# 1/rms by one power instruction and one Newton step, in a two-layer encoder kernel

## The chip, the cores and the metric

The kernel runs on one core of a Trainium2 chip. The metric is device time in microseconds (us) of one execution; the kernel before has a median of 1916.23 us over 3 runs (1915.28 to 1917.49). Engines are named as in the profile: PE (TensorE matmul; PEld is its weight load), DVE (VectorE), ACT (ScalarE), POOL (GpSimd), SP (SyncE, which here issues the DMAs).

## The reference

A trunk of two layers is applied to a prompt of 512 rows and a sample of 1024 rows, each row 1024 wide, with shared weights. Layer 0 has two attentions side by side (A: grouped queries with axial rotary; B: a difference of two softmaxes, with an RMS norm on its output). Layer 1 has one, C, with three dilated windows. Each layer:

```python
def rms_norm(x, g):
    x32 = x.astype(jnp.float32)
    y = x32 * lax.rsqrt(jnp.mean(x32 * x32, axis=-1, keepdims=True) + EPS)
    return (y * g.astype(jnp.float32)).astype(x.dtype)
...
    h = rms_norm(x, norm_g)
    z = h @ w_in                                   # q, k, v and a gate, split by columns
    q = partial_rope(rms_norm(q.reshape(B, S, C_HEADS, HEAD_DIM), c_q_norm))
    k = partial_rope(rms_norm(k.reshape(B, S, C_HEADS, HEAD_DIM), c_k_norm))
...
    return x + (o * jax.nn.silu(gate)) @ w_out
```

So 1/sqrt(mean + eps) is wanted in three places: once per row for h; once per row and head for q and k; and once per row and head for the output of B. All of it is float32 to the outside. EPS is 1e-6.

## The kernel before

**Tiles.** Rows are taken 128 at a time (12 tiles), and grouped in three granules of 4 tiles (`GRAN`: the prompt, and two halves of the sample). Activations and weights are split into a high and a low fp16 half, so that a product takes three fp16 passes (`PASSES`). h is written as such a pair, transposed by a DMA into `hT`, and kept for the whole layer. The layer is worked off in 8 units of two heads. For each unit and granule `kv_piece` and `qg_piece` project k, v and q, gate (48 matmuls per pair of tiles, PSUM tiles `pj`), and `att_A`, `att_B` or `att_C` do the attention: scores `S` on PE, maximum on DVE, exponential on ACT, high and low half on ACT and DVE, a transposing DMA `t<-h`, and the product with V on PE. `out_tile` is the output projection.

**1/rms.** Each of the three places takes the sum of squares, scales it and adds eps, makes a first guess by integer arithmetic on the bits of the number (a multiplication by -0.5 and an addition of a magic constant), and improves it with three Newton steps of four instructions each (`newton`, L261 to L264):

- h, per tile or pair of tiles (`l0_h`, and `fin0` for layer 1; tile name `hs4`): `h_var` on DVE (L363 and the guess at L256), then 12 instructions on POOL. For the very first tile all 14 are on DVE. `h_split` then multiplies the tile by 1/rms (DVE, L374), and splits it (ACT L379, DVE L383).
- q and k (`qk_stages`; tile name `qs`, 128 rows by 8 values), 87 times: `f_red` sums on DVE (L527), `f_chain` puts 16 instructions on POOL: the square of the weight scale (L532, its tile is `wiz`), scale and eps (L533), guess (L534), Newton, and the weight scale again (L537). DVE then multiplies (`f_rope`, L568, or `f_r`, L560 for A), ACT and DVE split, and a transposing DMA puts K or q in place.
- the output of B (`att_B`, `fin`; tile name `bf`, 128 by 4), 12 times: scale and eps (L1046), guess (L1047), Newton, and two more instructions, all on POOL.

**Weight chunks.** `wprep` loads 256 columns of weights, sums their squares on ACT, adds them over partitions on PE (L436), makes a power of two of it on DVE (`f_pw`; the inverse scale goes to `wiz`, L447), and splits the weights (ACT L471, DVE L476). 29 chunks belong to w_in0 and w_in1, 8 to the output weights.

**Order.** A planner (`Plan`) sets the order of all instructions. Every stage is added with an engine and an estimated duration, e.g. `add("POOL", 6.9, f_chain, [s])`; `Plan.run` plays the stages through with these durations, and emits a stage when the modelled engine becomes free and its inputs are ready. Each engine then runs its instructions in the emitted order, SP its DMAs too. So a changed duration in an `add` changes the order on all engines. The list `START` orders the ramp, `END` the last two units.

Of the kernel before, what the change touches and what calls it, by code (L numbers as in the profile page):

```python
# [13 lines left out]
I32 = mybir.dt.int32  # L14
# [198 lines left out]
def trunk_kernel(ctx: ExitStack, tc: tile.TileContext, A: dict, outs: list):  # L213
# [186 lines left out]
    def wprep(w, cols, ih=None, iz=None, kinds=("whl",), deps=(), keep=2):  # L400
# [47 lines left out]
        pw = add("DVE", 0.75, f_pw, [mm] if ih is None else [mm, box["gst", 0 if w is w0 else 1]], (), [pt])  # L448
# [66 lines left out]
    def qk_stages(zb, ztok, evs, iz, tabs, tdep, ti, kind, isq, dst, dst_acq, dst_use, swap, dst_dep=()):  # L515
# [9 lines left out]
        def f_red():  # L525
            b["s"] = small(32, "qs", 6)
            V.tensor_reduce(out=b["s"][:, 0:8], in_=b["t1"].rearrange("p h t d -> p (h t) d"), op=AD, axis=AX.X)  # L527
        s = add("DVE", dve(512), f_red, [s], (), [t1t])

        def f_chain():  # L530
            x = b["s"]
            G.tensor_scalar(out=x[:, 24:25], in0=iz(), scalar1=iz(), scalar2=1.0 / 64, op0=M, op1=M)  # L532
            G.tensor_scalar(out=x[:, 8:16], in0=x[:, 0:8], scalar1=x[:, 24:25], scalar2=EPS, op0=M, op1=AD)  # L533
            G.tensor_scalar(out=x[:, 16:24].bitcast(I32), in0=x[:, 8:16].bitcast(I32), scalar1=-0.5, scalar2=MAGIC,  # L534
                            op0=M, op1=AD)
            newton(G, x[:, 16:24], x[:, 0:8], x[:, 8:16])
            G.tensor_scalar(out=x[:, 0:8], in0=x[:, 16:24], scalar1=iz(), scalar2=4096.0, op0=M, op1=M)  # L537
        sr = add("POOL", 6.9, f_chain, [s])
# [86 lines left out]
    def kv_piece(u, gi):  # L625
# [68 lines left out]
        u.k_ready[gi] = qk_stages(zb, ztok, evs, lambda: u.kvw.iz[:, 0:1], lambda: u.ktab, u.tdep, t0, u.kind, False,  # L694
# [1028 lines left out]
```

## Time and profile before

| | |
|---|---|
| median of 3 runs | 1916.23 us |
| the profiled execution, its own time | 1908.2 us |
| its span (first to last instruction) | 1906.3 us |
| mean granted clock of TensorE | 0.958 |
| PE busy | 1675.6 us (88%) |
| DVE, ACT, POOL busy | 1324.2 (69%), 1213.3 (64%), 862.0 us (45%) |
| PE at the start | first weight sum at 11.51 us, first projection at 21.41 us |

The span is the time from the first instruction to the last in one profiled execution; the execution's own time is 1.9 us longer, and the median of the timed runs 8.0 us above that. PE is the busiest engine; what it idles (1906.3 - 1675.6 = 230.7 us) is made of waits for other engines and for DMAs.

### The profile page before, as it was taken

What the parts mean: (1) busy time and instruction counts of PE and PEld (TensorE: products, weight loads), DVE (VectorE), ACT (ScalarE), POOL (GpSimd) and SP (SyncE); (2) the same over time, 40 slices, a digit from 0 to 9 for tenths busy, and PEclk for the clock granted to TensorE, in tenths of its full rate; (3) what the DMA queues carried; (4) which work ended last, traced back from release to release, by engine and by line L of the source; (5) the groups of instructions that cost most, each with busy time, mean ns of one, the idle gap of its engine ahead of it and who ended that gap; (6) DMA issues with size and microseconds to landing.
All of it is one profiled execution on the core that took longest, in us unless ns stands there. A gap on an engine that the chain in (4) does not pass through costs nothing.

```text
span 1906.3 us, 45950 instructions
## 1 busy us (share of the span) xinstructions
PE 1675.6 (88%) x17626; PEld 1400.0 (73%) x17626; DVE 1324.2 (69%) x2976; ACT 1213.3 (64%) x2593; POOL 862.0 (45%) x2272
## 2 busy tenths in 40 slices
PE   4588889999988999786899998999998889894898
PEld 3475667778877877465788887878887778783787
DVE  5768878877787778974555768676866767687432
ACT  4548878876676677753435668576767657786310
POOL 3743434444555575523124445554554564463100
PEclk9898999999999999897999999999999999997999
DMA  8678999995564554579787568484858666777983
GB/s 244 147 141 149 168 178 171 152 170 125 96 133 74 104 114 103 123 182 203 200 192 168 101 122 170 105 178 102 167 114 154 123 119 130 153 140 156 216 221 111
DMA packets 788734, 282.14 MB, mean 148 GB/s; under 512 B 647073, under 2 KB 772257, under 8 KB 788513
## 3 DMA queue, kind: packets, MB, share of 16 engines
q1 hardware_dynamic: 788512, 279.19, 71.2%
q8 instruction: 138, 2.26, 0.5%
q14 instruction: 84, 0.68, 0.1%
HBM read 73.92 MB, written 25.17 MB: 52 GB/s over the span
## 4 chain that ended last, share of the span: by engine, by line
PE 49%; DMA 10%; DVE 9%; ACT 5%; POOL 4%; issue 4%; SPq 2%; DVEq 0%; POOLq 0%; ACTq 0%
PE pj L490 36%; DMA t<-h 7%; PE pj L785 5%; PE S L773 3%; DVE f L1100 2%; PE S L1125 2%; DMA f<-in_w_in_dram 1%; PE pj L504 1%; DVE h L801 1%; ACT f L1110 1%; DVE whl L476 1%; PE S L1173 1%; DVE qs L527 1%; SPq L358 1%; ACT f L1025 1%
## 5 line engine op out<-in xcount | busy, mean ns | idle before, releaser
L490 PE MATMUL pj<-whl,hT 128*128 128x256 f16 x7680 | 882.5, 275 | 34.7 <-DMA hT<-h 31.9
L490 PEld LDWEIGHTS <-hT 128*128 128x128 f16 x7968 | 781.1, 99 | 152.8 <-DMA hT<-h 33.7
L785 PEld LDWEIGHTS <-t 128*128 128x128 f16 x4992 | 204.4, 101 | 105.0 <-DMA t<-h 91.8
L490 PEld LDWEIGHTS <-t 128*128 128x128 f16 x2304 | 229.0, 100 | 54.2 <-DMA t<-h 24.1
L1110 ACT ACTIVATE f<-f,cs,csc 128x256 f32<-128x256 f32 (+1 forms) x384 | 218.8, 574 | 60.5 <-DVE cs L779 60.2
L801 DVE TENSOR_TENSOR h<-f,h 128x1024 f16<-128x1024 f32 x148 | 186.4, 1262 | 78.7 <-ACT h L797 77.5
L773 PE MATMUL S<-K,q 128*128 128x512 f16 x640 | 173.1, 404 | 61.1 <-ACT f L1025 29.4
L490 PE MATMUL pj<-whl,t 128*128 128x256 f16 x1728 | 202.1, 279 | 23.2 <-DMA t<-h 23.2
L785 PE MATMUL pj<-V,t 128*128 128x64 f16 (+1 forms) x4032 | 181.3, 204 | 38.4 <-DMA t<-h 37.9
L797 ACT ACTIVATE h<-f 128x1024 f16<-128x1024 f32 x168 | 176.1, 1054 | 13.2 <-DMA t<-h 9.9
L773 PEld LDWEIGHTS <-q 128*128 128x128 f16 x640 | 62.5, 103 | 122.5 <-issue 63.6
L533 POOL TENSOR_SCALAR qs<-qs 128x8 f32<-128x8 f32 x87 | 41.1, 473 | 218.6 <-DVE qs L527 208.3
L1335 DVE SCALAR_TENSOR_TENSOR f<-pj,os,f 128x256 f32<-128x256 f32 x96 | 41.9, 479 | 114.4 <-PE pj L490 114.0
L855 DVE TENSOR_REDUCE as<-S 128x1 f32<-128x1024 f32 (+1 forms) x80 | 96.5, 1219 | 22.4 <-PE S L773 22.1
L424 ACT ACTIVATE t<-f 128x1024 bf16<-128x1024 f32 x74 | 77.9, 1053 | 49.3 <-DMA f<-in_w_in_dram 32.6
L865 ACT ACTIVATE f<-S,as,asc 128x1024 f32<-128x1024 f32 (+1 forms) x96 | 101.7, 1061 | 11.2 <-DVE h L801 6.1
L476 DVE SCALAR_TENSOR_TENSOR whl<-f,wsm,whl 128x1024 f16<-128x1024 f32 x68 | 89.0, 1325 | 11.4 <-ACT whl L471 11.1
L801 POOL TENSOR_TENSOR h<-f,h 128x1024 f16<-128x1024 f32 x20 | 45.3, 2264 | 96.8 <-ACT h L797 42.6
L471 ACT ACTIVATE whl<-f,wsm 128x1024 f16<-128x1024 f32 x68 | 76.2, 1144 | 19.2 <-PE pj L490 18.8
L1019 DVE TENSOR_REDUCE bs<-S 128x1 f32<-128x1024 f32 x64 | 77.3, 1217 | 15.4 <-PE S L773 15.2
L655 ACT ACTIVATE z<-pj 128x256 f32<-128x256 f32 x78 | 29.3, 376 | 92.0 <-PE pj L490 91.9
L262 POOL TENSOR_TENSOR qs<-qs 128x8 f32<-128x8 f32 x261 | 74.0, 284 | 20.4
(253 smaller groups left out, 2955.5 us busy)
## 6 DMA issues: line engine op xcount, KB each, us to landing
f<-in_w_in_dram SPq DMA_DIRECT2D x58, 512.0 KB, 5.1
mixbuf<-sg SPq DMA_DIRECT2D x48, 256.0 KB, 2.7
f<-mixbuf SPq DMA_DIRECT2D x24, 512.0 KB, 5.1
K<-K SPq DMA_DIRECT2D x78, 128.0 KB, 2.8
f<-in_w_out_dram SPq DMA_DIRECT2D x16, 512.0 KB, 5.3
pn<-pk SPq DMA_DIRECT2D x96, 66.0 KB, 2.5
x1buf<-f SPq DMA_DIRECT2D x12, 512.0 KB, 4.3
Vc<-V SPq DMA_DIRECT2D x96, 64.0 KB, 2.4
```

The costliest lines, as they stand in the source:

```text
L424: S_.activation(out=junk1(t1t), in_=b[i].rearrange("p k n -> p (k n)"), func=AF.Square, accum_out=b["s"][:, i:i + 1])
L471: S_.activation(out=part(k, 0, i), in_=b[i][:, nk * k:nk * k + nk, :], func=AF.Copy, scale=sc())
L476: stt(out=part(k, 1, i), in0=b[i][:, nk * k:nk * k + nk, :], scalar=sc(), in1=part(k, 0, i), op0=M, op1=SU)
L490: T.matmul(ps, lhs(k, a), wt(k, b), start=(k == 0 and i == 0), stop=(k == 7 and i == 2))
L773: T.matmul(out[:, 512 * i:512 * i + 512], q, u.K[:, st, gi, hk, :], start=(st == 0), stop=(st == 1))
L785: T.matmul(o, t4[:, 8 * a + base + k, :], v(k, b), start=(k == 0 and i == 0), stop=(k == nk - 1 and i == 2))
L797: S_.activation(out=b["hl"][:, 0, :], in_=b["e"], func=AF.Copy)
L801: (G if on_pool else V).tensor_tensor(b["hl"][:, 1, :], b["e"], b["hl"][:, 0, :], SU)
L855: V.tensor_reduce(out=b["s"][:, 0:nh], in_=b["S"].rearrange("p (h k) -> p h k", h=nh), op=ALU.max, axis=AX.X)
L865: S_.activation(out=b["e"][:, w * i:w * i + w], in_=b["S"][:, w * i:w * i + w], func=AF.Exp, bias=b["s"][:, 2 + i:3 + i], scale=u.sc, accu ...
L1019: V.tensor_reduce(out=b["s"][:, c:c + 1], in_=b["S", c], op=ALU.max, axis=AX.X)
L1110: S_.activation(out=b["e"][:, w * i:w * i + w], in_=b["e"][:, w * i:w * i + w], func=AF.Exp, bias=b["s"][:, i:i + 1], scale=u.sc, accum_ou ...
```

## The change

The guess and three Newton steps become one `pow` with exponent -0.5 on POOL (a constant tile `mhalf` holds the exponent) and one Newton step. In q and k the weight scale no longer enters per piece: `f_pw` works out eps divided by the square of the scale (`c.e2`, two DVE instructions per chunk of w_in), and the chain becomes six instructions. The two instructions of `h_var` go from DVE to POOL, and the first tile's whole chain too. The durations given to the planner follow.

```diff
-    def newton(eng, y, t, v):
-        for _ in range(3):
-            eng.tensor_tensor(t, y, y, M)
-            eng.tensor_tensor(t, t, v, M)
-            eng.tensor_scalar(out=t, in0=t, scalar1=-0.5, scalar2=1.5, op0=M, op1=AD)
-            eng.tensor_tensor(y, y, t, M)
+    def rsqrt(y, t, v, n):
+        G.tensor_tensor(y, v, mhalf[:, 0:n], ALU.pow)
+        G.tensor_tensor(t, y, y, M)
+        G.tensor_tensor(t, t, v, M)
+        G.tensor_scalar(out=t, in0=t, scalar1=-0.5, scalar2=1.5, op0=M, op1=AD)
+        G.tensor_tensor(y, y, t, M)
...
-    def h_var(s, n, eng):
-        ts(out=s[:, 0:n], in0=s[:, 0:n], scalar1=1.0 / D, scalar2=EPS, op0=M, op1=AD)
-        seed(s[:, n:2 * n], s[:, 0:n])
-        if eng is not None:
-            newton(eng, s[:, n:2 * n], s[:, 2 * n:3 * n], s[:, 0:n])
+    def h_rms(s, n):
+        G.tensor_scalar(out=s[:, 0:n], in0=s[:, 0:n], scalar1=1.0 / D, scalar2=EPS, op0=M, op1=AD)
+        rsqrt(s[:, n:2 * n], s[:, 2 * n:3 * n], s[:, 0:n], n)
...
                 ts(out=c.iz, in0=s[:, 4:4 + n], scalar1=ih(), scalar2=1.0 / P14, op0=M, op1=M)
-        pw = add("DVE", 0.75, f_pw, [mm] if ih is None else [mm, box["gst", 0 if w is w0 else 1]], (), [pt])
+                c.e2 = small(1, "we2", 12)
+                V.reciprocal(out=s[:, 4:5], in_=c.iz[:, 0:1])
+                ts(out=c.e2, in0=s[:, 4:5], scalar1=s[:, 4:5], scalar2=EPS / 4096.0 ** 2, op0=M, op1=M)
+        pw = add("DVE", 1.1, f_pw, [mm] if ih is None else [mm, box["gst", 0 if w is w0 else 1]], (), [pt])
...
         def f_chain():
             x = b["s"]
-            G.tensor_scalar(out=x[:, 24:25], in0=iz(), scalar1=iz(), scalar2=1.0 / 64, op0=M, op1=M)
-            G.tensor_scalar(out=x[:, 8:16], in0=x[:, 0:8], scalar1=x[:, 24:25], scalar2=EPS, op0=M, op1=AD)
-            G.tensor_scalar(out=x[:, 16:24].bitcast(I32), in0=x[:, 8:16].bitcast(I32), scalar1=-0.5, scalar2=MAGIC,
-                            op0=M, op1=AD)
-            newton(G, x[:, 16:24], x[:, 0:8], x[:, 8:16])
-            G.tensor_scalar(out=x[:, 0:8], in0=x[:, 16:24], scalar1=iz(), scalar2=4096.0, op0=M, op1=M)
-        sr = add("POOL", 6.9, f_chain, [s])
+            G.tensor_scalar(out=x[:, 8:16], in0=x[:, 0:8], scalar1=1.0 / (64.0 * 4096.0 ** 2), scalar2=e2(), op0=M, op1=AD)
+            rsqrt(x[:, 0:8], x[:, 16:24], x[:, 8:16], 8)
+        sr = add("POOL", 3.6, f_chain, [s])
...
-                newton(G, x[:, 8:12], x[:, 12:16], x[:, 4:8])
+                rsqrt(x[:, 8:12], x[:, 12:16], x[:, 4:8], 4)
...
-            s = add("POOL", 5.9 + pool(512), f_ch, [s, u.sg_ready[gi], u.cst], (), [u.sgtok[gi]])
+            s = add("POOL", 3.2 + pool(512), f_ch, [s, u.sg_ready[gi], u.cst], (), [u.sgtok[gi]])
...
-        if tls[0] == 0 and g == 0:
-            s = add("DVE", 2.62, lambda: h_var(b["s"], n, V), sqs)
-        else:
-            s = add("DVE", 0.26, lambda: h_var(b["s"], n, None), sqs)
-            s = add("POOL", 4.6, lambda: newton(G, b["s"][:, n:2 * n], b["s"][:, 2 * n:3 * n], b["s"][:, 0:n]), [s])
+        s = add("POOL", 2.0 + 0.15 * n, lambda: h_rms(b["s"], n), sqs)
...
-        s = add("DVE", 0.26, lambda: h_var(b["s"], 1, None), [s])
-        s = add("POOL", 4.6, lambda: newton(G, b["s"][:, 1:2], b["s"][:, 2:3], b["s"][:, 0:1]), [s])
+        s = add("POOL", 2.2, lambda: h_rms(b["s"], 1), [s])
```

POOL's list goes from 2276 rows to 1209, and the order on the other engines changes with the durations. Two places in the ramp, before and now. On POOL, in the ramp, the kernel before ends the Newton steps of the second pair of sample tiles (`hs4_447`), and only then starts on the first K piece (`qs_417`):

```order
L261 TENSOR_TENSOR hs4_447<-hs4_447 128x2
L262 TENSOR_TENSOR hs4_447<-hs4_447 128x2
L263 TENSOR_SCALAR hs4_447<-hs4_447 128x2
L264 TENSOR_TENSOR hs4_447<-hs4_447 128x2
L532 TENSOR_SCALAR qs_417<-wiz_133 128x1
L533 TENSOR_SCALAR qs_417<-qs_417 128x8
L534 TENSOR_SCALAR qs_417<-qs_417 128x8
```

In the changed kernel the first K piece is `qs_401`, the first pair of sample tiles `hs4_174`, the second pair `hs4_429`, and `hz_475` half the gate's scale; the power stands at L260:

```order
L264 TENSOR_TENSOR hs4_174<-hs4_174 128x2
L741 TENSOR_SCALAR hz_475<-wiz_223 128x1
L534 TENSOR_SCALAR qs_401<-qs_401,we2_142 128x8
L260 TENSOR_TENSOR qs_401<-qs_401,mhalf_76 128x8
L261 TENSOR_TENSOR qs_401<-qs_401 128x8
L262 TENSOR_TENSOR qs_401<-qs_401 128x8
L263 TENSOR_SCALAR qs_401<-qs_401 128x8
L264 TENSOR_TENSOR qs_401<-qs_401 128x8
L363 TENSOR_SCALAR hs4_429<-hs4_429 128x2
```

The first K piece has moved ahead of the second pair of sample tiles.

On SP, in the ramp, the kernel before issues the tables of A's k (`akc`, `aks`) and of A's q (`aqg`, `aqc`, `aqs`), and then the transposition of the second prompt tile (`h41_233`) and, behind a load of a sample tile, of the third:

```order
L322 DMA akc_204<-in_cosA_dram 128x8x64
L322 DMA aks_206<-in_sinA_dram 128x8x64
L288 DMA aqg_236<-in_a_q_norm_dram 128x64
L322 DMA aqc_238<-in_cosA_dram 128x8x64
L322 DMA aqs_240<-in_sinA_dram 128x8x64
L387 DMA_TRANSPOSE hT00_170<-h41_233 128x16x128
L1540 DMA f43_255<-in_x_sample_dram 128x1024
L387 DMA_TRANSPOSE hT00_170<-h42_251 128x16x128
```

In the changed kernel:

```order
L322 DMA akc_188<-in_cosA_dram 128x8x64
L322 DMA aks_190<-in_sinA_dram 128x8x64
L385 DMA_TRANSPOSE hT00_161<-h41_183 128x16x128
L288 DMA aqg_227<-in_a_q_norm_dram 128x64
L322 DMA aqc_229<-in_cosA_dram 128x8x64
L322 DMA aqs_231<-in_sinA_dram 128x8x64
L385 DMA_TRANSPOSE hT00_161<-h42_220 128x16x128
```

The second tile's transposition has moved ahead of the three DMAs of A's q tables, and these now stand between it and the third tile's.

## Rows read from the trace of the kernel before

**Rows 1.** Windows view: busy us (instructions) per engine, clock, DMA; the ramp, then everything.
```profile
core 0: us, PE busy (x) PEld busy (x) DVE busy (x) ACT busy (x) POOL busy (x), PEclk, DMA share, GB/s
0.00:110.00 110.00, 58.98 (x426) 45.45 (x427) 70.12 (x140) 62.38 (x105) 55.17 (x137) 0.88 0.80 190
...
sum 1906.00, PE 1675.61 PEld 1400.01 DVE 1324.18 ACT 1213.34 POOL 862.00; mean PE 279.27 PEld 233.34 DVE 220.70 ACT 202.22 POOL 143.67
```

**Rows 2.** Timeline of PE, ramp: start, duration, instructions, [idle before <-what ended it].
```profile
34.02 20.28 PE L490 MATMUL pj<-whl,hT 128*128 128x256 f16 x168 [7.09 <-DMA hT<-h]
63.33 10.49 PE L490 MATMUL pj<-whl,hT 128*128 128x256 f16 x72 [9.02 <-DMA hT<-h]
...
77.11 2.79 PE L490 MATMUL pj<-whl,hT 128*128 128x256 f16 x24 [2.87 <-DMA hT<-h]
...
85.56 3.17 PE L773 MATMUL S<-K,q 128*128 128x512 f16 x7 [4.84 <-DMA K<-K]
```

**Rows 3.** Timeline of SP's queue, ramp: issues of tables and transpositions.
```profile
21.68 1.22 SPq L322 DMA_DIRECT2D aks<-in_sinA_dram  x1
...
26.88 4.76 SPq L387 DMA_TRANSPOSE hT<-h  x1
...
32.37 5.68 SPq L387 DMA_TRANSPOSE hT<-h  x2
```

**Rows 4.** Timeline of 45 to 70 us: first K piece's sum, POOL's chains.
```profile
45.07 0.69 DVE L527 TENSOR_REDUCE qs<-t 128x8 f32<-128x512 f32 x1
...
46.56 0.20 POOL L261 TENSOR_TENSOR hs<-hs 128x2 f32<-128x2 f32 x1 [2.83 <-DVE hs L256]
...
59.98 1.35 POOL L532 TENSOR_SCALAR qs<-wiz 128x1 f32<-128x1 f32 x1
...
69.06 0.27 POOL L537 TENSOR_SCALAR qs<-qs,wiz 128x8 f32<-128x8 f32 x1
```

**Rows 5.** Groups of POOL: xcount | busy us, mean ns | idle before.
```profile
L262 POOL TENSOR_TENSOR qs<-qs 128x8 f32<-128x8 f32 x261 | 74.0, 284 | 20.4
L264 POOL TENSOR_TENSOR qs<-qs 128x8 f32<-128x8 f32 x261 | 72.8, 279 | 21.7
L261 POOL TENSOR_TENSOR qs<-qs 128x8 f32<-128x8 f32 x261 | 72.4, 278 | 20.9
L263 POOL TENSOR_SCALAR qs<-qs 128x8 f32<-128x8 f32 x261 | 63.9, 245 | 23.3
L801 POOL TENSOR_TENSOR h<-f,h 128x1024 f16<-128x1024 f32 x20 | 45.3, 2264 | 96.8 <-ACT h L797 42.6 <-DVE den L883 22.2 <-DMA t<-h 14.0
...
L532 POOL TENSOR_SCALAR qs<-wiz 128x1 f32<-128x1 f32 x87 | 40.2, 462 | 8.2
...
L537 POOL TENSOR_SCALAR qs<-qs,wiz 128x8 f32<-128x8 f32 x87 | 35.1, 403 | 9.0
...
L534 POOL TENSOR_SCALAR qs<-qs 128x8 int32<-128x8 int32 x87 | 22.0, 253 | 7.6
```

**Rows 6.** Chain that ended last, in order of time: start, us, what.
```profile
385.41 0.28 POOL qs L533
...
387.96 0.07 issue
...
1725.51 0.05 POOL qs L263
```

**Rows 7.** Timeline at 390 us, POOL and DVE side by side.
```profile
390.78 2.63 POOL L801 TENSOR_TENSOR h<-f,h 128x1024 f16<-128x1024 f32 x1
391.46 2.19 DVE L574 TENSOR_TENSOR s<-t,bks 128x64 f32<-128x64 f32 x2
```

**Rows 8.** Groups of DVE, columns as in rows 5.
```profile
L574 DVE TENSOR_TENSOR s<-t,cqs 128x64 f32<-128x64 f32 x48 | 8.9, 227 | 0.8
...
L925 DVE RECIPROCAL bs<-bs 128x2 f32<-128x2 f32 x48 | 7.7, 160 | 16.2 <-ACT f L1025 8.3 <-ACT f L983 7.7
...
L447 DVE TENSOR_SCALAR wiz<-wsm,n1ih 128x2 f32<-128x2 f32 x16 | 3.7, 230 | 0.0
```

**Rows 9.** Timeline of PE behind a chain of B's output.
```profile
804.62 3.57 PE L773 MATMUL S<-K,q 128*128 128x512 f16 x8 [4.81 <-ACT f L1025]
```

More of the change, by code (lines that the diff above doesn't have):

```diff
@@ L512, in h_deps, with qk_stages @@
         return r
-    def qk_stages(zb, ztok, evs, iz, tabs, tdep, ti, kind, isq, dst, dst_acq, dst_use, swap, dst_dep=()):
+    def qk_stages(zb, ztok, evs, e2, tabs, tdep, ti, kind, isq, dst, dst_acq, dst_use, swap, dst_dep=()):
         b = {}
@@ L525, in f_red @@
         def f_red():
-            b["s"] = small(32, "qs", 6)
+            b["s"] = small(24, "qs", 6)
             V.tensor_reduce(out=b["s"][:, 0:8], in_=b["t1"].rearrange("p h t d -> p (h t) d"), op=AD, axis=AX.X)
@@ L693, in kdst @@
             return u.K[:, 0, gi]
-        u.k_ready[gi] = qk_stages(zb, ztok, evs, lambda: u.kvw.iz[:, 0:1], lambda: u.ktab, u.tdep, t0, u.kind, False,
+        u.k_ready[gi] = qk_stages(zb, ztok, evs, lambda: u.kvw.e2, lambda: u.ktab, u.tdep, t0, u.kind, False,
                                   kdst, [u.ktok] if gi == 0 else (), [u.ktok], lambda: u.K[:, 1, gi],
@@ L762, in qg_piece @@
         ti = row // 128 if u.kind == "C" else t0
-        u.q_ready[gi] = qk_stages(zb, ztok, evs, lambda: u.qgw.iz[:, 0:1], lambda: u.qtab, u.tdep, ti, u.kind, True,
+        u.q_ready[gi] = qk_stages(zb, ztok, evs, lambda: u.qgw.e2, lambda: u.qtab, u.tdep, ti, u.kind, True,
                                   qdst, (), [qt], None)
@@ L1046, in f_ch @@
                 G.tensor_scalar(out=x[:, 4:8], in0=x[:, 0:4], scalar1=u.kb2(), scalar2=EPS, op0=M, op1=AD)
-                G.tensor_scalar(out=x[:, 8:12].bitcast(I32), in0=x[:, 4:8].bitcast(I32), scalar1=-0.5, scalar2=MAGIC,
-                                op0=M, op1=AD)
-                newton(G, x[:, 8:12], x[:, 12:16], x[:, 4:8])
+                rsqrt(x[:, 8:12], x[:, 12:16], x[:, 4:8], 4)
                 G.tensor_scalar(out=x[:, 0:4], in0=x[:, 8:12], scalar1=u.kap(), scalar2=0.0, op0=M, op1=AD)
                 G.tensor_tensor(u.sg[gi], u.sg[gi], x[:, 0:4].unsqueeze(2).to_broadcast([128, 4, 128]), M)
-            s = add("POOL", 5.9 + pool(512), f_ch, [s, u.sg_ready[gi], u.cst], (), [u.sgtok[gi]])
+            s = add("POOL", 3.2 + pool(512), f_ch, [s, u.sg_ready[gi], u.cst], (), [u.sgtok[gi]])
             def f_m():
@@ L1343, in trunk_kernel @@
     V.memset(ones, 1.0)
+    mhalf = const(8, "mhalf")
+    V.memset(mhalf, -0.5)
     ln14 = const(1, "ln14")
```

## The prediction

> **What bounds the kernel now.** I read the windows view first. Over the whole span PE is busy for 1675.6 of 1906 us, so the most that any change off PE can win is some 230 us of idle time; 51 us of it (110 - 59) lie in the first 110 us, where PE works little more than half of the time [rows 1]. POOL is busy for 862 us, less than half: its throughput bounds nothing. What counts is how late its results are. So I went on to the timeline of PE in the ramp, then to the queue and the engine that end PE's waits there, and last to the chain that ended last, for the rest.
>
> Once PE has begun to project, four waits in the ramp are longer than 2.5 us: 7.09, 9.02, 2.87 and 4.84 us [rows 2]. The first ends with the transposition of the second prompt tile, which SP issues at 26.88 us, behind DMAs of tables [rows 3]. The second and third end with transpositions of sample tiles, whose h waits for 1/rms from POOL. The fourth ends with K, and K waits for POOL most of all: its sum of squares is ready at 45.76 us, POOL first does two chains for h (from 46.56 us), begins K's at 59.98 us and ends it at 69.33 us [rows 4].
>
> After 327 us (the chain of waits can be followed back that far) PE's waits are spread thin. The chain runs through pieces of the 1/rms work on POOL 124 times, in ten stretches, the first at 385.41 us and the last ending at 1725.56 us; the pieces are 0.05 to 2.3 us long and add up to 43.8 us, with 0.07 us of issue between two of them [rows 6].
>
> **The change part by part.**
>
> *The q and k chain.* From a chain of 16 go L532 (0.462 us), L534 (0.253), L537 (0.403) and two Newton steps of four, each 0.278 + 0.284 + 0.245 + 0.279 = 1.086 us [rows 5]; with the ten issue gaps of 0.07 that is 1.12 + 2.17 + 0.70 = 4.0 us. One power instruction of P us is added, and its place between two others is already counted.
>
> *P* is not in the trace. By operands and size its nearest row is a tensor_tensor of 128x8, 0.28 us; it can't cost less than that, since it is an instruction of the same form over the same data with more arithmetic. The far end is the costliest instruction that POOL has in the trace, 2.26 us for 128x1024 [rows 5]. I take 0.8 us, near the row of the same size but not on it, since a power is surely not one multiplication. So a chain gets 3.2 us shorter (3.7 to 1.7).
>
> A rule bears on P. The Trainium skill (Perfetto Trace Analysis, section Roofline) says that elementwise operations of GpSimd are bound by memory at about any arithmetic intensity. By that a power costs what a multiplication of the same tile costs; the trace has no power to agree or disagree, and the sum below would win 2.4 us more.
>
> *The ramp.* (a) The second prompt tile's transposition moves ahead of A's q tables on SP. It can be issued when `aks` is out, at 22.90 us, instead of 26.88 [rows 3]. But the three q table DMAs now stand before the third tile's, which was issued at 32.37 us: 22.9 + 4.8 for the second tile's + 1.5 to 3.8 for the tables puts it at 29.2 to 31.5, so PE, which needs that tile 2.6 us after the second, stops there instead. I count 1.5 us of the 4.0.
> (b) The first sample pair: the 12 POOL instructions from 46.56 us become six, and the two on DVE before them go. With 0.20 us and 0.07 us gap each, 12 x 0.27 = 3.2 and some stalls become 5 x 0.27 + P = 2.2. DVE also loses the two instructions of the next pair that stood in its queue ahead of the multiplication. I count 2.5 us together of the 9.02.
> (c) K's chain now stands ahead of the second sample pair's. It can start near 49 us and end near 52, so K is no longer what PE waits for at 85.56 us. Late next are the transpositions of the remaining sample tiles, at 4 to 5 us of SP's queue each. Of 2.87 + 4.84 = 7.7 us I count half, 4.
> Ramp: 1.5 + 2.5 + 4 = 8 us.
>
> *The rest.* Ten stretches on the chain times 3.2 us would be 32 us, and less where the chain holds only part of the 16 instructions: the saving can't be more than a share of 3.2/5.6 of 43.8, or 25 us. (5.6 = 16 instructions of rows 5's durations with gaps, without L532, which can run ahead of the sum.) Most of that isn't PE time: at 385 us PE goes on working while the chain stands on POOL, and what would be late next is a transposition or ACT. A stretch with a PE wait right behind it is the one of B's output at 797 to 804 us, where PE idles for 4.81 us [rows 9]; there a Newton chain of 128x4 precedes the gate's multiplication. I count 7 of the 25.
>
> *DVE.* In 29 chunks a reciprocal (0.16 us, the row of 128x2) and a tensor_scalar with two scalars (0.23) are added [rows 8], 11 us in all. They stand between the sum of squares and the weights' rounding, and their cover is that a chunk is prepared a unit ahead; in the ramp PE waits for hT at that time, not for weights. Without that cover each costs 0.4 us, at most 11. The two h instructions that leave DVE, and the first tile's chain, about make up for it (the first tile goes from 14 DVE to 6 POOL instructions of similar total). I count +0.5.
>
> *Sum* against the profiled execution: span 1906.3 - 8 - 7 + 0.5 = 1891.8; the execution's own time 1908.2 becomes 1893.7. The median shown is 1916.23, 8.0 above the profiled one, so I forecast 1901.7, rounded 1902.
>
> **The rivals.**
>
> *A slow power, on the other side.* Place: POOL's queue, and DVE beside it. With P above 4.0 a chain is longer than before. And a long POOL instruction holds DVE: while POOL ran its 2.63 us at 390.78, two small DVE operations took 2.19 us, against 0.23 each elsewhere [rows 7, 8]. The Trainium skill has it too: Advanced Engine Details and Errata, section Mode Summary, says that GpSimd and two-port VectorE instructions block each other on a shared port; the trace agrees, with 2.19 us. At P = 5 each of some 15 chains on PE's path (ten late, five in the ramp) would cost 1 us more and hold DVE's next operation for up to 0.3 of that again: 1916 + 20 = 1936. Against it: no small POOL row is anywhere near 4 us.
>
> *The new order loses.* The planner emits another order for every engine, from a first difference in PE's list in the ramp. Two new waits of the size of those in rows 2 and 9 (9 and 5 us) at bad places would take the 14.5 back and more: 1916 - 14.5 + 20 = 1922. For it: every engine's queue is in order, and one misplaced DMA cost 4 us at 22.90. Against: the planner's rules are the same.
>
> *Hidden anyway.* PE's waits are taken over by the next late thing, transpositions above all, and only a few us remain: 1914.
>
> *More is won.* If all of (b) and (c) goes, 9.0 + 7.7 and 1.5 for (a), and 15 of the 25 later: 18 + 15 = 33, less 0.5, is 1884.
>
> **How the numbers follow.** My forecast has 0.49 (its own range 1892 to 1911), more is won 0.20, hidden anyway 0.12, the new order loses 0.12, a slow power 0.07. The range goes down to 1884, to hold half of the second case, and up to 1920, to hold the hidden case and part of the fourth; P's ends alone move the sum by 7 us up (25 becomes 13, and the ramp a little less) and 2.4 down, within it. About 0.2% (3.8 us) is what a measurement of this kernel can tell from no change. Faster by more than that: 0.49 + 0.20 + 0.03 of the hidden case = 0.72. Same: 0.10. Slower: 0.18.
>
> **What would show it.** POOL's busy time falls: without the gaps a q or k chain loses 3.3 - P = 2.5 us, 87 of them 217 us, the 30 others some 60, so from 862 to about 585 us; if it falls to 530, P is near 0.28; if it stays above 700, P is near 2. The first scores of the sample's K and q come 5 us or more earlier than 80 to 85 us; PE's busy time in the first 110 us rises by about 8; the wait before the second prompt tile shrinks and a new one stands before the third. PE's total busy time stays within some us of 1675. The forecast is wrong if the ramp wins but later stretches give it back (the new order), or if DVE's small operations grow beside the power (the slow one).

## The result and the profile after

The changed kernel takes 1867.52 us (median of 4 runs, 1862.99 to 1870.77), the kernel before 1915.76 us (4 runs beside it): a ratio of 0.9748, 95% interval 0.9723 to 0.9773. It is faster by 48 us, where 14.5 were forecast and the range ended at 1884. The profiled execution took 1870.77 us, with a span of 1868.5.

The windows view of the kernel after, against [rows 1]:

```profile
core 0 of [0], span 1868.5 us
core 0: us, PE busy (x) PEld busy (x) DVE busy (x) ACT busy (x) POOL busy (x), PEclk, DMA share, GB/s
0.00:110.00 110.00, 63.39 (x449) 49.03 (x450) 71.85 (x135) 62.63 (x104) 47.84 (x81) 0.84 0.85 197
```

and the page's line of busy times (us, share of the span, instructions):

```profile
PE 1671.1 (89%) x17626; PEld 1399.3 (75%) x17626; DVE 1345.7 (72%) x2985; ACT 1211.2 (65%) x2593; POOL 692.3 (37%) x1204
```

PE does 4.4 us more by 110 us (counted in columns, it has done by 106 us what it had done by 110), and its total is nearly that of before, at nearly the same mean granted clock (0.957, before 0.958). What went is its idle time: span less busy time was 230.7 us and is 197.4. POOL has lost 170 us, not 277.

The timelines of the ramp, SP's queue and then PE, against [rows 3] and [rows 2]:

```profile
22.41 1.04 SPq L322 DMA_DIRECT2D aks<-in_sinA_dram  x1
23.54 5.25 SPq L385 DMA_TRANSPOSE hT<-h  x1
...
29.94 0.58 SPq L322 DMA_DIRECT2D aqs<-in_sinA_dram  x1
30.62 6.45 SPq L385 DMA_TRANSPOSE hT<-h  x2
```

```profile
30.40 5.18 PE L491 MATMUL pj<-whl,hT 128*128 128x256 f16 x24 [2.50 <-DMA hT<-h]
36.47 2.79 PE L491 MATMUL pj<-whl,hT 128*128 128x256 f16 x24 [0.90 <-DMA hT<-h]
40.35 13.27 PE L491 MATMUL pj<-whl,hT 128*128 128x256 f16 x120 [1.08 <-DMA hT<-h]
60.12 8.29 PE L491 MATMUL pj<-whl,hT 128*128 128x256 f16 x48 [6.50 <-DMA hT<-h]
...
70.04 2.79 PE L491 MATMUL pj<-whl,hT 128*128 128x256 f16 x24 [1.51 <-DMA hT<-h]
74.45 2.79 PE L491 MATMUL pj<-whl,hT 128*128 128x256 f16 x24 [1.62 <-DMA hT<-h]
...
81.16 3.17 PE L771 MATMUL S<-K,q 128*128 128x512 f16 x7 [3.69 <-DMA K<-K]
```

The second prompt tile comes 3.6 us earlier, the wait for the first sample pair is 6.50 instead of 9.02 us, and K's scores start 4.4 us earlier.

The groups of POOL (columns as in [rows 5]), and the spread of the power over its sizes (ns: least, median, most):

```profile
L260 POOL TENSOR_TENSOR qs<-qs,mhalf 128x8 f32<-128x8 f32 x87 | 147.6, 1696 | 7.3
L534 POOL TENSOR_SCALAR qs<-qs,we 128x8 f32<-128x8 f32 x87 | 43.0, 495 | 340.6 <-DVE qs L528 320.7 <-DVE wsm L256 17.1
L261 POOL TENSOR_TENSOR qs<-qs 128x8 f32<-128x8 f32 x87 | 28.4, 327 | 6.8
L262 POOL TENSOR_TENSOR qs<-qs 128x8 f32<-128x8 f32 x87 | 26.7, 306 | 6.8
L263 POOL TENSOR_SCALAR qs<-qs 128x8 f32<-128x8 f32 x87 | 24.3, 280 | 7.8
L264 POOL TENSOR_TENSOR qs<-qs 128x8 f32<-128x8 f32 x87 | 21.1, 242 | 7.3
```

```profile
L260 POOL TENSOR_TENSOR qs<-qs,mhalf x87: 1637/1645/2584, 49.8 to 1692.0; 128x8 f32<-128x8 f32 x87
L260 POOL TENSOR_TENSOR hs<-hs,mhalf x19: 547/552/766, 8.0 to 985.3; 128x1 f32<-128x1 f32 x14, 128x2 f32<-128x2 f32 x5
L260 POOL TENSOR_TENSOR bf<-bf,mhalf x12: 1011/1017/2054, 480.7 to 882.3; 128x4 f32<-128x4 f32 x12
```

The middle line mixes two sizes. So P, the power of 128x8, has a median of 1.65 us and a mean of 1.70, in the upper half of its bounds. The six means and five gaps of 0.07 make a q or k chain of 3.7 us. It got shorter by the 4.0 us that the prediction takes from [rows 5] less 1.70: by 2.3 us, not 3.2.

**Where the 48 us come from.** Adding up the columns of the matmul rows of a trace, in order of time, gives the moment at which PE has done a given share of its work, and so how long each share took. Four pieces of the work are enough: up to 12% of the columns (the ramp and what follows, to 293 us before), 12 to 40% (to 794), 40 to 44% (to 902: the change of layer), and the rest. Here are the profiled executions that the text below needs, in us, and with each the busy time of PE and the mean granted clock of TensorE:

```
                                       0-12%   12-40%   40-44%   44-100%   PE busy   clock
before                                 292.9    501.1    108.4     998.6    1675.6   0.958
after                                  278.8    506.2     88.5     990.0    1671.1   0.957
e1   new instructions, old order       291.9    497.8    107.7     997.6    1675.4   0.954
e2   old instructions, new order       290.0    546.4     91.4     998.3    1680.9   0.954
e3   no Newton step, after's order     278.6    495.1     87.9     977.7    1655.5   0.967
e4   power twice, after's order        281.1    538.3     89.3     998.8    1682.8   0.955
e5   planner told of q/k only          294.6    499.2     95.8     985.5    1673.7   0.954
e6   planner told of all but q/k       278.7    507.6     84.5     990.8    1667.8   0.962
e7   planner told, q/k 5.2             282.7    493.6     90.4     985.6    1662.9   0.962
e9   before, load 1.9                  301.4    514.8    102.7     997.5    1685.7   0.947
e10  e1, load 1.9                      300.5    510.2    105.8     994.6    1681.9   0.948
e11  old instructions, q/k 6.0         295.0    515.3     90.6     983.3    1672.5   0.956
e12  planner told of h only            293.9    502.3    106.7     992.2    1674.6   0.957
e13  after, load 1.9                   287.1    506.9     90.9     987.0    1672.6   0.954
e14  planner told of h and B           294.4    496.1     96.0    1009.8    1682.7   0.950
e15  planner told of h and the chunk   275.6    506.4    107.6     981.2    1670.5   0.961
e16  e11, load 1.9                     306.7    516.1     89.2     991.7    1683.2   0.954
e17  old instructions, chunk 1.1       294.5    515.4     96.8     992.7    1678.3   0.956
e18  old instructions, both            298.9    503.5    114.8     988.4    1683.1   0.951
```

The change wins 14 us up to 12%, gives 5 back up to 40%, wins 20 at the change of layer and 9 behind it. That makes 38 us and not 48: the two profiled executions are only 37 us apart (1908.2 and 1870.8 us), the medians 48. A wait of about 5 us for scores stands just behind the 40% mark before and just ahead of it after (4.81 and 5.37 us, in the rows below), so that much of the 5 given back and of the 20 won is one wait on either side of the mark.

All these kernels run the same 17626 matmuls, and PE's busy time for them still goes from 1655.5 to 1685.7 us, by and large the more, the lower the granted clock. Between before and after only 4.5 us are of this kind. Between others it can be much of the difference, which is said where it matters; why the clock differs was not traced.

The first thing to learn was whether the shorter chains win the time, or the order that the planner makes of their durations.

### The profile page after: what moved, and what is told of

Same layout as the page of the kernel before. It is cut to its first block, busy times and chain, and to the rows that moved or that the text cites. A ratio compares the mean times of both kernels' runs of the same rounds, so it can differ in the third digit from the quotient of the medians.

```text
span 1868.5 us, 44772 instructions
## 1 busy us (share of the span) xinstructions
PE 1671.1 (89%) x17626; PEld 1399.3 (75%) x17626; DVE 1345.7 (72%) x2985; ACT 1211.2 (65%) x2593; POOL 692.3 (37%) x1204
## 3 DMA queue, kind: packets, MB, share of 16 engines
q8 instruction: 138, 2.26, 0.5%
## 4 chain that ended last, share of the span: by engine, by line
PE 46%; DVE 10%; DMA 10%; POOL 6%; ACT 5%; issue 4%; SPq 0%; DVEq 0%; POOLq 0%; ACTq 0%
PE pj L491 35%; DMA t<-h 9%; PE pj L783 4%; PE pj L505 2%; PE S L1121 2%; DVE f L1096 2%; PE S L771 2%; POOL qs L260 1%; DVE h L799 1%; PE S L1169 1%; ACT f L1106 1%; DVE bs L1017 1%; DVE f L934 1%; ACT f L981 1%; DVE t L566 1%
## 5 line engine op out<-in xcount | busy, mean ns | idle before, releaser
L799 DVE TENSOR_TENSOR h<-f,h 128x1024 f16<-128x1024 f32 x148 | 199.6, 1352 | 43.5 <-ACT h L795 43.2
L771 PE MATMUL S<-K,q 128*128 128x512 f16 x640 | 168.9, 397 | 51.4 <-ACT f L1023 21.0
L534 POOL TENSOR_SCALAR qs<-qs,we 128x8 f32<-128x8 f32 x87 | 43.0, 495 | 340.6 <-DVE qs L528 320.7
L260 POOL TENSOR_TENSOR qs<-qs,mhalf 128x8 f32<-128x8 f32 x87 | 147.6, 1696 | 7.3
L1331 DVE SCALAR_TENSOR_TENSOR f<-pj,os,f 128x256 f32<-128x256 f32 x96 | 42.0, 479 | 108.9 <-PE pj L491 108.4
L477 DVE SCALAR_TENSOR_TENSOR whl<-f,wsm,whl 128x1024 f16<-128x1024 f32 x68 | 94.3, 1400 | 6.4 <-ACT whl L472 6.3
L1096 DVE CUSTOM_DVE_ANT_0 f<-S,mask 128x256 f32<-128x256 f32 x192 | 69.7, 421 | 25.3 <-PE S L1169 25.3
L799 POOL TENSOR_TENSOR h<-f,h 128x1024 f16<-128x1024 f32 x20 | 43.4, 2172 | 117.3 <-ACT h L795 104.3
L585 ACT ACTIVATE st<-t 128x512 f16<-128x512 f32 x87 | 54.2, 623 | 48.6 <-DVE t L579 32.1
```

What stands on the lines that cost most here:

```text
L260: G.tensor_tensor(y, v, mhalf[:, 0:n], ALU.pow)
L477: stt(out=part(k, 1, i), in0=b[i][:, nk * k:nk * k + nk, :], scalar=sc(), in1=part(k, 0, i), op0=M, op1=SU)
L771: T.matmul(out[:, 512 * i:512 * i + 512], q, u.K[:, st, gi, hk, :], start=(st == 0), stop=(st == 1))
L799: (G if on_pool else V).tensor_tensor(b["hl"][:, 1, :], b["e"], b["hl"][:, 0, :], SU)
L1096: V.tensor_tensor_reduce(out=b["e"][:, w * i:w * i + w], in0=b["S"][:, w * i:w * i + w], in1=mask(x), scale=1.0, scalar=-3.0e38, op0=AD, o ...
```

## The experiments

Ratios are to the kernel before in the same rounds, with 95% intervals; 0.01 of a ratio is 19 us. The median of the kernel before was 1910.0 to 1912.7 us in these rounds and 1915.8 in those of the result, so differences of medians between rounds are good to some us. Where the two ways of comparing disagree, both are given. The numbers given to the planner (the second argument of `add`) only set the order in which each engine's instructions are written.

**e1, e2: instructions and order apart.** e1 has the new instructions with the planner's old numbers, and every engine's order is that of before but for the instructions exchanged; e2 has the old instructions with the new numbers.

```diff
# e1: after, with the numbers of before; e2 is before, with those of after
...
-        pw = add("DVE", 1.1, f_pw, [mm] if ih is None else [mm, box["gst", 0 if w is w0 else 1]], (), [pt])
+        pw = add("DVE", 0.75, f_pw, [mm] if ih is None else [mm, box["gst", 0 if w is w0 else 1]], (), [pt])
-        sr = add("POOL", 3.6, f_chain, [s])
+        sr = add("POOL", 6.9, f_chain, [s])
-            s = add("POOL", 3.2 + pool(512), f_ch, [s, u.sg_ready[gi], u.cst], (), [u.sgtok[gi]])
+            s = add("POOL", 5.9 + pool(512), f_ch, [s, u.sg_ready[gi], u.cst], (), [u.sgtok[gi]])
-        s = add("POOL", 2.0 + 0.15 * n, lambda: h_rms(b["s"], n), sqs)
...
+            s = add("DVE", 0.26, None, sqs)
+            s = add("POOL", 4.6, lambda: h_rms(b["s"], n), [s])
...
```

> The changed kernel's instructions, but the planner is given the durations and stages of the kernel before, so PE, ACT and SP run exactly the order of before, and DVE and POOL too but for the instructions exchanged. Theory L (shorter chains on POOL give the time): most of the 48 us, 1870 to 1885 us. Theory O (the planner's new order gives it): only what the prediction summed for shorter chains, about 1900 us.

> The instructions of before (seed and three Newton steps, weight scale in each chain), but the planner is given the changed kernel's durations, so PE, ACT and SP run exactly the changed kernel's order. Theory L: as slow as before or slower, 1910 to 1930 us. Theory O: most of the gain without one faster instruction, 1875 to 1890 us.

e1: 1904.78 us, 0.9985 (0.9962 to 1.0008). e2: 1935.40 us, 1.0138 (1.0115 to 1.0160). The chains that are 2.3 us shorter are worth 3 us in the old order, and that is not told from nothing (the interval goes from 7 us won to 2 lost); the new order with the old chains loses 26; both together win 48. Neither half holds the gain: it is an interaction. The waits of DVE on a q/k chain of POOL show a part of it (total us, times, longest). Before, e1, e2 and after, in this order:

```profile
DVE t L568 <- POOL qs L537: 38.6, 22, 4.0
```

```profile
DVE t L566 <- POOL qs L264: 6.9, 9, 1.6
```

```profile
DVE t L568 <- POOL qs L537: 108.5, 68, 3.9
```

```profile
DVE t L566 <- POOL qs L264: 24.7, 30, 2.7
```

In e1 the result is there in time: DVE's wait falls from 38.6 to 6.9 us, but what reads it still stands where it stood in DVE's queue, behind other work, and PE hardly notices. In e2 the reader stands early, and 68 times DVE's head of the queue waits for POOL with all that stands behind it. What such waits cost depends on the place. Against after, which has the same order, all of DVE's waits for q/k chains grow from 9 to 44 us between 293 and 836 us, and e2 takes 40 us longer from 12 to 40%; behind 930 us they grow from 15 to 69, and from 44% on e2 takes only 8 us longer.

The change of layer is another matter. There the chain of waits that ends PE's longest wait (start, us, what), of before (`x1buf<-f` stores a tile of x1, and L374 then multiplies the same tile in place by 1/rms):

```profile
847.65 6.45 DMA x1buf<-f
...
854.20 1.30 DVE f L374
...
856.60 1.23 DVE h L383
857.83 0.80 DVE f L1335 x2
...
859.80 1.05 ACT h L1289
...
860.87 1.29 DVE h L1294
...
862.22 6.56 DMA t<-h
```

and PE's waits there, of before, e1 and after:

```profile
804.62 3.57 PE L773 MATMUL S<-K,q 128*128 128x512 f16 x8 [4.81 <-ACT f L1025]
...
826.68 1.87 PE L773 MATMUL S<-K,q 128*128 128x512 f16 x4 [3.07 <-ACT f L1025]
...
868.83 7.89 PE L490 MATMUL pj<-whl,t 128*128 128x256 f16 x48 [11.26 <-DMA t<-h]
...
898.78 8.27 PE L490 MATMUL pj<-whl,t 128*128 128x256 f16 x48 [6.34 <-DMA t<-h]
```

```profile
800.31 3.47 PE L771 MATMUL S<-K,q 128*128 128x512 f16 x8 [4.81 <-ACT f L1023]
...
863.84 7.87 PE L491 MATMUL pj<-whl,t 128*128 128x256 f16 x48 [11.20 <-DMA t<-h]
...
893.76 8.26 PE L491 MATMUL pj<-whl,t 128*128 128x256 f16 x48 [6.33 <-DMA t<-h]
```

```profile
784.21 3.57 PE L771 MATMUL S<-K,q 128*128 128x512 f16 x8 [5.37 <-ACT f L1023]
...
840.56 2.50 PE L783 MATMUL pj<-V,t 128*128 128x128 f16 x24 [2.70 <-DMA t<-h]
...
858.45 6.81 PE L491 MATMUL pj<-whl,t 128*128 128x256 f16 x48 [7.77 <-DMA t<-h]
```

No 1/rms of POOL stands on that chain. DVE's line 374 waits for the store of x1, which SP issues at 847.65 us and which has read the tile at 854.10; the output's work (1335, 1289, 1294) stands behind it. With shorter chains in the same order (e1) the two long waits are the same to 0.06 us. With the new order PE's waits are another set. In this piece those for a transposition before a projection fall from 17.6 us to 7.8, and those for an exponential before scores from 13.6 to 4.7 (the 5.37 us at 784.21 stand ahead of the mark). PE gets through the piece in 88.5 us instead of 108.4, and with the new order and the *old* chains (e2) in 91.4. So 17 of the 20 us come with the order alone. It is not the wait of DVE for a store of x1 that went. In before, and then in after, where it is longer:

```profile
854.20 1.28 DVE L374 SCALAR_TENSOR_TENSOR f<-f,hs,V 128x1024 f32<-128x1024 f32 x1 [4.67 <-DMA x1buf<-f]
```

```profile
844.61 1.28 DVE L372 SCALAR_TENSOR_TENSOR f<-f,hs,V 128x1024 f32<-128x1024 f32 x1 [11.07 <-DMA x1buf<-f]
```

Which difference of the two orders makes PE wait less here was not tested.

**e3, e4: the length of the chain, in after's order.** e3 leaves out the Newton step (the power alone makes 1/rms; four instructions fewer), e4 computes the power twice.

```diff
# e3
         G.tensor_tensor(y, v, mhalf[:, 0:n], ALU.pow)
-        G.tensor_tensor(t, y, y, M)
-        G.tensor_tensor(t, t, v, M)
-        G.tensor_scalar(out=t, in0=t, scalar1=-0.5, scalar2=1.5, op0=M, op1=AD)
-        G.tensor_tensor(y, y, t, M)
# e4
+        G.tensor_tensor(t, v, mhalf[:, 0:n], ALU.pow)
         G.tensor_tensor(y, v, mhalf[:, 0:n], ALU.pow)
```

> The changed kernel in its own order, the Newton step left out: four POOL instructions fewer in each of the 118 chains, about 1.4 us per q or k chain (327 + 306 + 280 + 242 ns and four gaps of 0.07). Theory L: the change shortened a q or k chain by 2.3 us and won 48 us, so 1.4 us more should win 20 to 30 us: 1838 to 1848 us. Theory O: the order is the same, so 3 to 10 us: about 1860 us.

> The changed kernel in its own order, each power computed a second time into the scratch of the Newton step: 1.7 us more in a q or k chain, 1.1 in B's, 0.6 in h's, and as much more time in which POOL can hold VectorE. Theory L: 25 to 35 us lost, 1893 to 1903 us. Theory O: 5 to 12 us lost, about 1876 us.

e3: 1848.07 us, 0.9678 (0.9661 to 0.9694). e4: 1914.74 us, 1.0031 (1.0018 to 1.0043). A chain longer by a power and its gap, 1.8 us, costs 47 us by the medians and 54 by the ratios; one shorter by four small instructions, 1.4 us (their means and gaps), wins another 19 or 13. So in this order a microsecond of q/k chain (those of h and B change with it) goes with 10 to 14 us when it gets shorter and 26 to 30 when it gets longer; in the old one (e1: 3 us for 2.3) with about 1.3. Not all of this is waiting: of the 24 us between the profiled spans of after and e3 16 are PE's busy time, at a granted clock of 0.967 instead of 0.957; of the 44 us between after and e4 it is 12. e4's DVE waits as e2's does:

```profile
DVE t L567 <- POOL qs L265: 96.2, 59, 4.5
```

**e5, e6, e7, e12, e14, e15: which number of the planner.** All have the new instructions. e5 tells the planner of the q/k chain only; e6 of everything but that (6.9 stays); e7 plans it at 5.2; e12 tells of the h chains only, e14 also of B's output, e15 of h and the weight chunk.

```diff
# e5: after, with e1's numbers except
         sr = add("POOL", 3.6, f_chain, [s])
# e6 (e7 has 5.2)
-        sr = add("POOL", 3.6, f_chain, [s])
+        sr = add("POOL", 6.9, f_chain, [s])
# e12: after, with the old 0.75, 6.9 and 5.9; e14 is e12 with the new 3.2 for B; e15 is e12 with
         pw = add("DVE", 1.1, f_pw, [mm] if ih is None else [mm, box["gst", 0 if w is w0 else 1]], (), [pt])
```

> The changed kernel's instructions; the planner is given 3.6 us for the q and k chain, and everything else (h, B's output, weight chunk) as before. Theory T (each engine's order puts the reader of a chain's result where the planner thought it ready; a shorter chain pays only if the planner is told): the q and k chain is the one that VectorE waits for (44.7 us before), so most of the gain, 1870 to 1885 us against 1905 for the same instructions with all durations of before. Rival R (the new order is a lucky draw of the whole plan): any other order is another draw, about 1900 us.

> The changed kernel's instructions and durations, but the planner is given 6.9 us for the q and k chain, as before. Theory T: the ramp's share of the gain and little else, 1890 to 1900 us. Rival R: another draw, about 1900 us too, or anything from 1870.

> The changed kernel, the planner given 5.2 us for the q and k chain, half way between 6.9 and 3.6. Theory T: about half of the gain, 1880 to 1893 us. Rival R: a draw that has nothing to do with the halves, 1865 or 1905 as well.

> The changed kernel's instructions; the planner is told of the shorter h chain alone (2.0 + 0.15 n and 2.2 us), and has 6.9 us for q and k, 5.9 for B, 0.75 for a weight chunk as before. Theory T: the ramp's 10 to 14 us, and what the layer change (12 h chains) gives: 1875 to 1892 us. Rival R: another draw, 1865 to 1905 us; it is told apart by where the time comes from, the ramp or elsewhere.

> The changed kernel's instructions; the planner is told of the shorter chains of h and of B's output, not of q and k's (6.9 us) nor of the weight chunk's (0.75). With h alone it was 1905 us, with h, B and the weight chunk 1869. If B's duration carries the difference: 1865 to 1880 us. If it is the weight chunk's: about 1905 us. Rival R: anything between 1860 and 1920.

> The changed kernel's instructions; the planner is told of h's shorter chain and of the weight chunk's 1.1 us, not of q and k's (6.9 us) nor of B's (5.9). If the weight chunk's duration carries the difference: 1865 to 1880 us. If it is B's: about 1905 us. Rival R: anything between 1860 and 1920.

```
e5   1887.56 us  0.9875 (0.9841 to 0.9909)     e12  1905.04 us  0.9968 (0.9952 to 0.9984)
e6   1868.56 us  0.9770 (0.9737 to 0.9804)     e14  1903.57 us  0.9955 (0.9935 to 0.9974)
e7   1860.18 us  0.9736 (0.9707 to 0.9764)     e15  1878.67 us  0.9838 (0.9815 to 0.9862)
```

My theory that the q/k number carries the gain fell with e6: without it nothing is lost. Nor need DVE's readers stand early for the gain, since in e6 DVE waits for the chains as little as in e1:

```profile
DVE t L566 <- POOL qs L264: 5.6, 8, 1.5
```

So the waits of e2 and e4 show what a long chain costs in after's order, not what the gain is made of. B's number beside that for h is worth nothing (e14), and 5.2 for q/k (e7) is as good as 3.6. The number for the weight chunk on DVE, 0.75 to 1.1 us, which I had not weighed at all, is worth 26 us beside that for h (e12 to e15), and the table shows where: of these kernels, those with 1.1 take 276 to 283 us for the first 12%, those with 0.75, and e1, 292 to 295. With old instructions it does nothing there (e17: 294.5). The q/k number alone (e5) wins nothing in the ramp, 13 us at the change of layer and 13 behind it.

**e9, e10, e13, e16: is it luck?** If any new order may be 30 us better or worse, the result says nothing on the durations. So another number, that of a load, goes from 1.85 to 1.9 in four kernels: before (e9), e1 (e10), after (e13), e11 (e16).

```diff
-T_DMA = 1.85
+T_DMA = 1.9
```

> The kernel before, unchanged but for one number that has nothing to do with the change: the planner's duration of a load, 1.9 us instead of 1.85. That gives another order on every engine from the ramp on. Theory T (the gain needs shorter chains and a plan that knows of some of them): 1900 to 1925 us. Rival R (the order of before is a poor draw, and nearly any other order gains, at the layer change and late in layer 1): 1870 to 1895 us.

> The changed kernel's instructions, all durations of the chains as before, and the load's duration 1.9 instead of 1.85 us: the order of the run before in this call, with the short chains. Theory T: as with the order of before, 1895 to 1908 us. Rival R: 1865 to 1890 us, and as much below the kernel before as the other order's run with the old instructions or a little more.

> The changed kernel with the planner's load duration at 1.9 us instead of 1.85, as in e9 and e10. Theory T (shorter chains that the plan knows of): far below e10, which has the same instructions and the same load duration but the chains' old durations: 1870 to 1890 us. Rival R (the changed kernel's order is a lucky draw): 1900 to 1925 us, as e10.

> The kernel before with 6.0 us planned for the q and k chain (1891 us in e11) and the load duration 1.9. If the 20 us of e11 come from the truer duration: 1895 to 1908 us, that much below e9 (1924). If e11 was a lucky order: 1910 to 1930 us.

```
e9   1924.22 us  1.0064 (1.0043 to 1.0085)     e13  1876.74 us  0.9820 (0.9804 to 0.9837)
e10  1920.74 us  1.0039 (1.0024 to 1.0054)     e16  1904.76 us  0.9969 (0.9952 to 0.9986)
```

Such a nudge alone makes each of them slower, by 9 to 16 us in the medians and 10 to 14 in the ratios. In all four 8 to 12 us of it lie in the first 12%, and a part is PE's busy time (e9: 10 us more than before, at a clock of 0.947), so these are four measurements of one nudge, not four draws. But the change still wins: with the new load number the changed kernel (e13) is 47 us below the old one (e9), and 44 below new instructions with old numbers (e10), which again gain only 3 us on e9. So a lucky order of after alone does not explain the gain; ten-odd us of its size can be luck.

**e11, e17, e18: truer numbers for the old instructions.** In the trace of before a q/k chain takes about 6 us, not 6.9 (e11 plans 6.0), and the chunk's scale on DVE 0.84 us from the start of its first small operation (L256 at 12.13 us) to the end of its last (L447, 12.97), not 0.75 (e17 plans 1.1). e18 has both.

```diff
-        sr = add("POOL", 6.9, f_chain, [s])
+        sr = add("POOL", 6.0, f_chain, [s])
```

> The kernel before with 6.0 us planned for the q and k chain instead of 6.9, which is what it takes in the trace. Theory T: 1900 to 1915 us. Rival R: another draw, 1870 to 1935 us.

> The kernel before, where only the duration that the planner has for a weight chunk's scale on DVE is 1.1 us instead of 0.75; no instruction changes, their order does. If a truer plan wins by itself (theory: the chunk's stage takes 0.84 us in the trace, and 0.75 emits it too late), 1890 to 1905 us, since beside the h chains the same number won 26 us. If it wins only with shorter chains, or was a lucky order, 1910 to 1930.

> As the one before, and a q or k chain planned with 6.0 us instead of 6.9 (its real length is about 6). If the two truer durations add up with old instructions (20 us for q and k alone were measured), 1870 to 1885 us, and then the faster chains themselves are worth little more than the plan. If they don't add up, 1890 to 1915.

e11: 1891.13 us, 0.9895 (0.9866 to 0.9923). e17: 1906.48 us, 0.9966 (0.9950 to 0.9982). e18: 1912.56 us, 1.0006 (0.9992 to 1.0019). They don't add up: 20 and 7 us alone, none together, since e18's change of layer takes 114.8 us instead of 90.6. The 20 us of e11 are there with the new load number too (e16 against e9), so one number wins them with no faster instruction; but the two together don't give the old instructions what the change gives. That no order could is not shown: e6's, which keeps the old q/k number and wins as much as the changed kernel, was not run with the old instructions. The seven orders tried with the old instructions lie between 1891 and 1935 us, on the mean 1913 (1915.8, 1935.4, 1924.2, 1891.1, 1904.8, 1906.5, 1912.6), where the kernel before lies itself; the four with the new instructions and all or most of the new numbers (after, e6, e7, e13) lie at 1860 to 1877.

**e8: the fastest.** The power alone, without the Newton step, with the planner told of that (q/k 2.4, B 2.1, h 0.9 + 0.15 n and 1.1).

```diff
# e3, with
-        sr = add("POOL", 3.6, f_chain, [s])
+        sr = add("POOL", 2.4, f_chain, [s])
```

> The Newton step left out as in the run with the power alone (1848 us), and the planner told of it: 2.4 us for the q and k chain, 2.1 for B's, 0.9 + 0.15 n and 1.1 for h. Theory T: the readers move forward by 1.2 us, and a further 10 to 20 us are won: 1828 to 1838 us. Rival R: another draw, 1840 to 1870 us.

1841.99 us, 0.9637 (0.9598 to 0.9675): 25 us below the changed kernel by the medians, 21 by the ratios. The 6 us from e3 to e8, which would be the plan's, are not clear of the noise (1846.2 to 1850.5 us in e3, 1835.7 to 1847.8 in e8).

## Why the prediction was wrong

The direction was right, the size was not: 48 us instead of 14.5.

**The step that failed** is "The rest": "I count 7 of the 25". It priced the shorter chain by the pieces of 1/rms on the chain of waits of the kernel before, and thus in the order of before. In that order the saving is worth 3 us (e1), less than counted. But the kernel isn't left in that order. I had taken the new order only as a rival that loses ("Against: the planner's rules are the same"). With it the same instructions win 48 us, and behind the first 110 us, where I had counted these 7, the profiled execution wins 33 of its 37. The runs show what the order does: at the change of layer it wins 17 us by itself (e2); with the new chains the chunk's number wins 18 in the first 12% (e12 to e15); and the old chains lose 68 us against the new ones in it (e2 against after, 75 by the ratios). Readers that stand earlier in DVE's queue fit this loss, but e6 wins as much without them, so which places of the order the gain needs stays open.

**The stretch behind B's output** was the wrong place to look: the wait of 4.81 us [rows 9], which I put behind a Newton chain, is 4.81 in e1 too and 5.37 in after. The 20 us of the change of layer came from the two long waits for a transposition (11.26 and 6.34 us before, 7.77 in after), which I had not read and whose chain holds no 1/rms of POOL, and from the waits for exponentials, which the shorter chains alone hardly move (13.6 us before, 12.2 in e1).

**P** was taken at 0.8 us and is 1.65, inside the bounds of 0.28 to 2.26, at twice the value. POOL's busy time, 692 us, is just under the mark of 700 that I had named for "P near 2"; 87 x (1.70 - 0.80) = 78 of the 107 us between it and the forecast 585 are this.

**The ramp** went as described, at half its size: PE did 4.4 us more in the first 110 us, not 8. (a) The second prompt tile came 3.6 us earlier and the waits for it and the next are 2.50, 0.90 and 1.08 us where 7.09 stood, so 2.6 us were won and 1.5 counted; the stop that I had expected before the third tile is small, and its transposition went out at 30.62 us as worked out. (b) 2.5 us of the 9.02 were won, as counted. (c) is what failed: of 2.87 + 4.84 us I counted 4 as won, and 1.51, 1.62 and 3.69 stand there now, 0.9 less. K still ends the last, since its chain on POOL ran from 48.53 to 55.36 us, not to 52. By 12% of the work the gain was 14 us, but of these e1 has 1 and e2 3: they too need order and chains together.

**DVE**: the reciprocal and the scalar of 29 chunks cost 164 and 214 ns, 11 us, as counted. All of DVE grew by 21.5 us, 13 of them in the subtractions that make the low half of the exponentials (148 x 0.09):

```profile
L799 DVE TENSOR_TENSOR h<-f,h 128x1024 f16<-128x1024 f32 x148 | 199.6, 1352 | 43.5 <-ACT h L795 43.2
```

against a mean of 1262 ns before. It is not the power that holds them: the 4 that ran beside one took 1221 ns, as did those beside which POOL ran nothing. 22 took over 1.4 us (6 before), each beside one of POOL's own operations of 128x512 or 128x1024 (L1235, L1236, L799), and the means go with the order (1264 in e1, 1345 in e4): it is the new order that brings these together.

**The rivals.** "More is won" came nearest, and fell short by 17 us: it too priced the later stretches by the order of before. "The new order loses" is a real mechanism: it decides when the chain stays long (e2, and e4 at 5.5 us a chain). "Hidden anyway" is what e1 shows for the instructions alone. "A slow power": at 1.65 us it is far from the 4 us above which a chain would be longer than before, and the rows above show no operation of DVE held by it; in the new order one power more already takes all the gain (e4).

What stays open: which of two orders is the better one can't be told from their numbers. Orders that differ by a nudge of a load lie 9 to 16 us apart, and e18 shows two good numbers that spoil each other. Why the chunk's number helps the ramp only with the new chains was not traced. Whether e6's order, made with the old q/k number, would win with the old instructions was not run.

## What to carry to other kernels

Where a planner or a scheduler writes in-order queues, a faster operation is two changes, its instructions and the order made from its new duration; run each alone before you explain a result, and don't price the second by the operation's share of the old chain. A reader moved forward in an in-order queue wins only if its input really comes by then, so the duration given to the planner must not be too short: here each microsecond by which the chain exceeded what was planned went with some 26 to 32 us (e4: 47 to 54 for 1.8; e2 against after: 68 to 75 for 2.4). Too long a number for the q/k chain cost nothing (e6, e7). And before a gain of a few tens of microseconds is put down to a mechanism, nudge an unrelated number and see how far that alone moves the time (here 9 to 16 us), and look whether the waits or the granted clock moved.

## What the runs showed of the hardware

- A power on POOL costs by its elements, unlike the small operations around it: 550 ns (median) at 1 element per partition, 704 at 2, 1017 at 4, 1645 at 8, which is some 390 ns and 157 more for each element. A multiplication of the same tiles has medians of 195, 195, 202 and 203 ns (least, median, most; the second line has both 1 and 2 elements):

```profile
L261 POOL TENSOR_TENSOR qs<-qs x87: 200/203/1307, 52.4 to 1693.8; 128x8 f32<-128x8 f32 x87
L261 POOL TENSOR_TENSOR hs<-hs x19: 193/195/673, 8.7 to 985.9; 128x1 f32<-128x1 f32 x14, 128x2 f32<-128x2 f32 x5
L261 POOL TENSOR_TENSOR bf<-bf x12: 200/202/907, 481.8 to 883.3; 128x4 f32<-128x4 f32 x12
```

  So the rule weighed in the prediction, that of the Trainium skill (Perfetto Trace Analysis, section Roofline), does not hold for this operation as it was taken there: by it the power of 128x8 would cost what the multiplication does, and it costs eight times that.
- POOL's small operations stretch beside some large ones of DVE. Timeline of the ramp of after, POOL and DVE side by side, with the first K piece's chain:

```profile
48.53 1.20 POOL L534 TENSOR_SCALAR qs<-qs,we 128x8 f32<-128x8 f32 x1
49.81 2.48 POOL L260 TENSOR_TENSOR qs<-qs,mhalf 128x8 f32<-128x8 f32 x1
52.38 1.28 POOL L261 TENSOR_TENSOR qs<-qs 128x8 f32<-128x8 f32 x1
53.73 1.06 POOL L262 TENSOR_TENSOR qs<-qs 128x8 f32<-128x8 f32 x1
54.88 0.20 POOL L263 TENSOR_SCALAR qs<-qs 128x8 f32<-128x8 f32 x1
```

```profile
48.31 2.49 DVE L372 SCALAR_TENSOR_TENSOR t<-t,hs,V 128x1024 f32<-128x1024 f32 x2 [0.92 <-POOL hs L264]
...
52.37 2.36 DVE L381 TENSOR_TENSOR h<-t,h 128x1024 f16<-128x1024 f32 x2 [1.24 <-ACT h L377]
```

  While DVE ran two multiplications of 128x1024 (L372) and then two subtractions (L381), four POOL instructions took 1.20, 2.48, 1.28 and 1.06 us, where their medians are 0.27, 1.65, 0.20 and 0.20, and the next small one took 0.20 as soon as DVE was through. It is [rows 7] from the other side, and fits K's chain taking 6.8 us instead of 3.7. Whether the TENSOR_TENSORs of [rows 7] are of the two-port kind that the prediction speaks of, no run here shows. Not every large operation does it. Of the small Newton instructions in the trace of after, the 193 beside which DVE ran nothing took 192 to 207 ns, the 42 that ran only beside a maximum of 128x1024 (`TENSOR_REDUCE`) 198 to 206, and the 19 that ran only beside a subtraction of 128x1024 had a median of 1195.
